# SWA's first low parts behind the first half's maxima, and four rows scaled by GpSimd at the end, in a one-core encoder step

## The chip, the cores and the metric

The kernel runs on one core of a Trainium2 chip. The metric is the device time of one execution in microseconds (us). Three runs of the kernel before took 2179.26, 2181.84 and 2182.01 us; their median is 2181.84 us. A separate execution was profiled: it took 2183.19 us, and its first and last instruction lie 2181.1 us apart. This distance is called the span, and all places in the trace are given in us from its start.

The engines are called by the profile's names: PE is TensorE (PEld its weight loads), DVE is VectorE, ACT is ScalarE, POOL is GpSimd, and SP is SyncE, which here only issues DMAs.

## The reference, cut to what matters

One step of an encoder layer for 1024 prompt tokens and 64 sample tokens (1088 in all) with 1024 features, in float32:

```
xn = rms_norm(x)
A  = retention(xn) ...                       # 4 heads, rms_norm, swish gate, w_ret_out
B  = sliding_window_attention(xn) ...        # 16 heads of 64, chunks of 64, w_swa_out
x += (sigmoid(gate_a) * A + sigmoid(gate_b) * B) @ w_mix_out
mk, mv = rms_norm(mem) @ w_mk, rms_norm(mem) @ w_mv
x += cross_attention(rms_norm(x), mk, mv)
x += (silu(h @ w_gate) * (h @ w_up)) @ w_down       # h = rms_norm(x)
y  = x * rsqrt(mean(x * x) + eps) * g_final
```

Two pieces of this matter here. In the sliding-window attention (SWA) each chunk's scores get a bias, their maximum is taken, and exp, sum and division follow. In the last line, every token's sum of squares over all 1024 features has to be there before any element of y is.

## The kernel before, in words

Features lie on the 128 partitions, as eight tiles (k = 0 to 7) of 1088 token columns. Each float32 operand of the large products is split into two fp32r parts: a high part, which is a rounded copy made by ACT, and a low part, the rest, which DVE gets by a subtraction. A product then takes three matmuls: high by high, high by low, low by high (`mm3`, lines 156 to 158; `multiply`, lines 212 to 215). The phases come one after the other: projections with retention, SWA, merging, cross-attention, and the feed-forward net, whose last part (`down`, `finish`) makes y.

The order of the instructions on each engine is fixed when the kernel is built. A scheduler places them by their place in the source; `issue_after(x)` keeps what is in its block behind the instruction x in that order, `in_order` (line 911) puts PE's work behind the last matmul, and `queued` (line 1630) does the same for DVE. An engine works off its own order strictly, and so do the DMA queues that SP, ACT and POOL issue: what stands behind a waiting instruction waits too. Tiles come from pools with a few buffers, and who takes a buffer again waits for its last reader.

**The start of SWA.** There are 17 chunks in two halves each (`swa`, `halves`). `scores` multiplies on PE (line 972), takes bias and maximum on DVE (L982, four units with an accumulator each), prepares the sinks' part on DVE (L986), and exponentiates on ACT (L988, and L990 for the sinks). Then DVE adds and inverts the denominators (L991, L992) and POOL scales (L994). `turn` transposes on PE (L949 for values, L1011 for weights), `weigh` multiplies with the values (L1035). For each half `self.marks` keeps a pair: the sinks' part on DVE and the exponential of it on ACT. The list is filled as the halves are written down, so `marks[-1]` is that of the newest half, and `marks[0]` that of the first.

Between the halves, pieces of other products fill PE. `filler` (from line 1151) gives them out: first the last head of the memory values (two token tiles, 24 matmuls each, scaled by a factor per token at line 1167, stored by POOL's DMAs at L1168 and L1169), then the product of the retention output with `w_ret_out`, for which eight gated tiles of 384 columns (`ret`) and the first weights (`wq`) need high and low parts. `first_loads` has made their high parts on ACT (L1108, L1112); `first_low` makes the ten low parts on DVE (L1120). It is called at the start of `filler`, when two halves of scores have been written down. Behind it stand the next weights (L123 on ACT and L124 on DVE), and each finished product is multiplied by its gate on DVE (L1196), which also frees its PSUM buffer, of which there are two.

**The end.** The 1088 columns form three groups: c = 0 and c = 1 with 272 columns each, and c = 2 with 544, whose sums are finished first. `finish` has 16 products left, eight for c = 0 and eight for c = 1. After each, `grow` adds it to its row of y on DVE (L1654) and ACT squares it (L1658); `gather` adds up the squares (L1663). For each group, `sums` adds over the partitions on PE with a matrix of ones (L1672), `roots` makes the factor per token (four small steps on DVE and a square root on ACT, L1757 to L1764), `spread` brings it to all partitions on PE (L1690) and ACT copies it to `rstd` (L1694). Then a row is scaled and stored in one of two ways:

- `scale`: DVE multiplies by gain and factor in one instruction (L1700), for c = 0 and most of c = 1 with the factor straight from PSUM;
- `gain` and `aside`: ACT multiplies by the gain (L1705), POOL by the factor from `rstd` (L1709).

Of group 2, rows 0 to 6 go the first way, between the products of c = 1, and row 7 the second. Of group 1, three rows go the second way. Stores are issued by SP, those of group 1 in turn by SP and ACT. Products, sums and spreads take PSUM from a pool of four bank pairs.

Of the kernel before, what the change touches and what calls it, by code (L numbers as in the profile page):

```python
# [11 lines left out]
F32 = mybir.dt.float32  # L12
F32R = mybir.dt.float32r
AF = mybir.ActivationFunctionType
ALU = mybir.AluOpType
# [4 lines left out]
P = 128  # L20
# [89 lines left out]
class Kernel:  # L110
# [616 lines left out]
    def bank(self, name):  # L727
        return self.pr.tile([P, 2, BLK], F32, tag="r", name=name)
# [386 lines left out]

    def first_low(self):

        with self.tc.issue_after(self.marks[-1][0]):
            for a, hi, lo in self.first:
                self.nc.vector.tensor_tensor(out=lo, in0=a, in1=hi.bitcast(F32), op=ALU.subtract)  # L1120

# [29 lines left out]
    def filler(self):  # L1151

        nc, tc, io = self.nc, self.tc, self.io
        if True:
            ld, rets = self.ld, self.rets
            self.first_low()
            us, h = self.first_units, H - 1
            for t in range(2):
                ps = self.dense_psum()
                for k in range(KT):  # L1160
                    x = self.ms[k][:, :, t * P:(t + 1) * P]
                    self.mm3(ps[:, :256], x[:, 0], x[:, 1], *us[k // 4][k % 4], k == 0, k == KT - 1)
                    if k == 3:
                        yield
                o = ld()[:, :256]
                with tc.high_priority():
                    self.values_out = nc.scalar.mul(o, ps[:, :256], self.mtok[:, t:t + 1]).ins
                nc.gpsimd.dma_start(self.d_mv[h, :, t, :], o)  # L1168
                nc.gpsimd.dma_start(io["o_mv"][t * P:(t + 1) * P, h * 256:(h + 1) * 256], o)  # L1169
                yield  # L1170
            self.mem.close()
            self.pw2 = self.mem.enter_context(tc.tile_pool(name="pw2", bufs=2, reuse_waits="tile", side="right"))
            with tc.issue_after(self.values_out):
                units = {0: self.first_out, 1: self.unit(io["w_ret_out"][1], KT)}
            order = [(m, c) for c in range(3) for m in range(2)] + [(m, c) for m in range(2, KT) for c in range(3)]
            halves = [range(4), range(4, KT)]
            extra = {2: (1, 0), 3: (1, 1), 5: (2, 0), 7: (2, 1)}
            step = 0
            for m, c in order:
                c0, n = CH[c]  # L1180
                if m not in units:
                    if m == 2:
                        with tc.issue_after(first[0]), tc.issue_after(first[1]):
                            units[m] = self.unit(io["w_ret_out"][m], KT)
                    else:
                        units[m] = self.unit(io["w_ret_out"][m], KT)
                u, g = units[m], ld()
                self.load(g[:, :n], self.d_gate[1][m, :, c0:c0 + n])
                for ps in self.pieces(u, rets, c0, n):
                    if step in extra:  # L1190
                        i, j = extra.pop(step)
                        self.later_operands(*CH[i], halves[j])
                    step += 1
                    if ps is None:
                        yield
                ins = nc.vector.tensor_tensor(out=g[:, :n], in0=ps, in1=g[:, :n], op=ALU.mult).ins  # L1196
                if step == 6:
                    first = self.marks[-1]
                self.store(self.d_mix[m, :, c0:c0 + n], g[:, :n])
                yield  # L1200
# [434 lines left out]
    def finish(self, y, rest):  # L1635
# [29 lines left out]
        def sums(c, *more):  # L1665
# [8 lines left out]
            r = self.np.tile([P, 5], F32, tag="rf", bufs=2, name="rs_f")[:, :len(spans)]  # L1674
            factors[c] = r, spans, ps[:, :, 0]

        def roots(c, between=None):
            r, spans, ps = factors[c]
            v = self.np.tile([P, 5], F32, tag="vf", bufs=2, name="rf_v")[:, :len(spans)]
            t = self.np.tile([P, 5], F32, tag="tf", bufs=2, name="rf_t")[:, :len(spans)]  # L1680
            self.steps(r, v, t, ps, between)
# [21 lines left out]
        def gain(c, k):  # L1703
            o = y[k][:, cols[c]]
            nc.scalar.mul(o, o, self.gains[:, 3, k:k + 1])  # L1705

        def aside(c, k, queue=nc.sync):
            o = y[k][:, cols[c]]
            nc.gpsimd.tensor_tensor(out=o, in0=o, in1=self.rstd[:, cols[c]], op=ALU.mult)  # L1709
            queue.dma_start(self.io["o_y"][k, :, cols[c]], o)  # L1710

        for j in range(2 * KT):
# [10 lines left out]
            if j == KT + 3:  # L1723
                self.in_order(lambda: sums(0))
                roots(0)
            if j == KT + 6:
                pb0 = self.in_order(lambda: spread(0, False))[:, :HC]
            if c and m < KT - 1:
                scale(2, m)
            if c and KT - 5 < m < KT - 1:  # L1730
                gain(1, rest[m][0])
            if j == 2 * KT - 2:
                gain(2, KT - 1)
                aside(2, KT - 1)
        m = rest[-1][0]
        spare = [rest[i][0] for i in range(KT - 4, KT - 1)]
        scale(0, 0, pb0)
        scale(0, 1, pb0)
        self.in_order(lambda: sums(1, squares[1, m]))
        roots(1, lambda: scale(0, 2, pb0))  # L1740
        for k in range(3, KT):
            scale(0, k, pb0)
# [91 lines left out]
```

## Time and profile before

| what | value |
| --- | --- |
| median of three runs | 2181.84 us |
| the profiled execution | 2183.19 us, span 2181.1 us |
| busy share of the span | PE 98%, DVE 71%, ACT 40%, POOL 30% |
| mean granted PE clock | 0.995 |
| bytes moved by DMA | 290.84 MB |
| first and last score matmuls of SWA | 809.3 and 970.8 us |
| PE's waits from 808 to 980 us, after the profile | 4.2 us |
| products of `finish` on PE | from 2143.8 to 2167.3 us |
| last DVE and POOL instruction ends | about 2176.9 us |

A row of the timeline gives the start, the duration, the engine, the line, the operation, the tiles written and read with their shapes, and a count where like instructions were merged. A bracket tells how long the engine had stood idle before, and what ended it. A row of the windows gives, for one stretch, the busy time of PE, PEld, DVE, ACT and POOL, the granted PE clock as a share of full speed, the busy share of the DMA engines and what they moved. Durations of one instruction include its latency, so the starts of neighbours tell the pace better.

### The profile page before, as it was taken

To read this page: it belongs to the slowest core of one execution; us is meant where nothing else is said; L and a number is where in the kernel's file an instruction comes from. 1 tells how busy PE (TensorE), PEld (TensorE's weight loads), DVE (VectorE), ACT (ScalarE), POOL (GpSimd) and SP (SyncE) were. 2 spreads that over 40 slices of the span, in tenths; PEclk is the share of its full clock that TensorE was granted. 3 is DMA by queue.
4 is the path that set the end of the run, shared out by engine and by line. 5 is a ranking of instruction groups with operands and counts; after the bars stand their busy time and mean duration, and the time that the engine had idled before them with its cause. 6 is when DMAs were issued, how large, how long until landed. Compare 5 with 4: busy or idle time off the path is not lost. (4 is left out here: it accounts for less than half of the span.)

```text
span 2181.1 us, 41848 instructions
## 1 busy us (share of the span) xinstructions
PE 2142.3 (98%) x16389; PEld 2089.0 (96%) x16389; DVE 1553.4 (71%) x2824; ACT 876.4 (40%) x1898; POOL 651.7 (30%) x498
## 2 busy tenths in 40 slices
PE   8999999999999999999999999999999999999997
PEld 8999999999999997889999999999999999999997
DVE  8996868776687658665455555768777777787688
ACT  7344424344344447553233333333322322344343
POOL 1223233342344214430000000014565555514531
PEclk9999999999999999999999999999999999999999
DMA  6434354435344467326443111422333323294433
GB/s 208 154 131 114 114 152 125 137 111 159 103 160 164 166 206 246 118 80 219 124 155 120 40 49 59 146 87 91 121 124 116 105 96 120 94 331 128 135 107 119
DMA packets 181446, 290.84 MB, mean 133 GB/s; under 512 B 40290, under 2 KB 109314, under 8 KB 181250
## 3 DMA queue, kind: packets, MB, share of 16 engines
q1 hardware_dynamic: 176130, 278.18, 40.1%
q10 hardware_dynamic: 4608, 8.36, 1.0%
q8 instruction: 129, 2.11, 0.4%
q0 software_dynamic: 512, 1.64, 0.2%
q14 instruction: 67, 0.55, 0.1%
HBM read 196.95 MB, written 91.16 MB: 132 GB/s over the span
## 5 line engine op out<-in xcount | busy, mean ns | idle before, releaser
L124 DVE TENSOR_TENSOR wq<-raw,wq 128x512 fp32r<-128x512 f32 (+1 forms) x499 | 443.9, 893 | 134.8 <-ACT wq L123 131.4
L123 ACT CAST wq<-raw 128x512 fp32r<-128x512 f32 (+1 forms) x499 | 303.1, 614 | 567.1 <-PE pq L215 223.3
L212 PE MATMUL pq<-T,wq 128*128 128x272 f32 x1832 | 492.0, 288 | 4.9 <-ACT wq L123 3.3
L213 PE MATMUL pq<-T,wq 128*128 128x272 f32 x1832 | 492.9, 289 | 0.0
L213 PE MATMUL pq<-B,wq 128*128 128x272 f32 x1592 | 428.2, 289 | 2.9 <-DVE B L124 2.6
L212 PE MATMUL pq<-B,wq 128*128 128x272 f32 x1592 | 426.6, 288 | 0.5 <-ACT B L123 0.5
L190 POOL TENSOR_TENSOR raw<-raw 128x512 f32<-128x512 f32 (+1 forms) x59 | 86.0, 1458 | 1036.5 <-DVE rs_r L301 483.0
L215 PE MATMUL pq<-T,wq 128*128 128x272 f32 x1832 | 382.8, 289 | 1.5 <-DVE wq L124 1.5
L212 PEld LDWEIGHTS pq<-T,wq 128*128 128x128 f32 x1832 | 345.0, 188 | 6.7 <-ACT wq L123 3.1
L213 PEld LDWEIGHTS pq<-T,wq 128*128 128x128 f32 x1832 | 344.9, 188 | 1.2 <-issue 1.1
L215 PE MATMUL pq<-B,wq 128*128 128x272 f32 x1592 | 332.2, 289 | 0.0
L213 PEld LDWEIGHTS pq<-B,wq 128*128 128x128 f32 x1592 | 299.5, 188 | 4.3 <-DVE B L124 4.2
L212 PEld LDWEIGHTS pq<-B,wq 128*128 128x128 f32 x1592 | 299.4, 188 | 1.4 <-ACT B L123 0.9
L215 PEld LDWEIGHTS pq<-T,wq 128*128 128x128 f32 x1832 | 290.2, 190 | 2.6 <-DVE wq L124 1.8
L215 PEld LDWEIGHTS pq<-B,wq 128*128 128x128 f32 x1592 | 252.2, 190 | 0.5 <-issue 0.4
L259 DVE TENSOR_TENSOR u<-pq,u 128x544 f32<-128x544 f32 x177 | 127.2, 719 | 95.5 <-PE pq L215 95.4
L193 POOL TENSOR_TENSOR raw<-raw 128x512 f32<-128x512 f32 (+1 forms) x59 | 80.8, 1370 | 91.4 <-DVE wq L124 81.5
L598 DVE TENSOR_TENSOR stage<-pq,u 128x544 f32<-128x544 f32 x112 | 80.3, 717 | 36.9 <-PE pq L215 32.4
L191 POOL TENSOR_TENSOR raw<-raw 128x512 f32<-128x512 f32 (+1 forms) x59 | 88.8, 1505 | 3.6
L196 POOL TENSOR_TENSOR raw<-raw 128x512 f32<-128x512 f32 (+1 forms) x59 | 84.0, 1423 | 4.4
L1483 POOL TENSOR_TENSOR stage<-stage,rstd_f 128x544 f32<-128x544 f32 x40 | 63.9, 1607 | 39.1 <-ACT stage L1482 39.1
L156 PE MATMUL pd<-xc,wq 128*128 128x256 f32 (+1 forms) x256 | 74.5, 291 | 0.0
(383 smaller groups left out, 4548.4 us busy)
## 6 DMA issues: line engine op xcount, KB each, us to landing
hl<-d_op SPq DMA_DIRECT2D x85, 272.0 KB, 5.3
d_qkv<-stage SPq DMA_DIRECT2D x44, 272.0 KB, 2.7
d_op<-stage SPq DMA_DIRECT2D x44, 272.0 KB, 2.1
d_op<-ht SPq DMA_DIRECT2D x44, 272.0 KB, 3.3
raw<-w_gate SPq DMA_DIRECT2D x22, 512.0 KB, 3.6
raw<-w_up SPq DMA_DIRECT2D x22, 512.0 KB, 4.0
raw<-w_down SPq DMA_DIRECT2D x16, 512.0 KB, 4.8
d_gate<-stage ACTq DMA_DIRECT2D x28, 272.0 KB, 3.0
```

The source lines that it names most:

```text
L123: self.last_cast = self.nc.scalar.copy(hi, src).ins
L124: return self.nc.vector.tensor_tensor(out=lo, in0=src, in1=hi.bitcast(F32), op=ALU.subtract).ins
L156: mm(ps, wh, xh, start=start, stop=False)
L190: tt(out=a11, in0=a11, in1=a21, op=sub)
L191: tt(out=a21, in0=a21, in1=a22, op=add)
L193: tt(out=a11, in0=a22, in1=a11, op=sub)
L196: tt(out=a12, in0=a12, in1=a11, op=sub)
L212: mm(ps[:, c, :HC], w[:, 0, ks], x[:, 0, cs], start=start, stop=False)
L213: mm(ps[:, c, :HC], w[:, 0, ks], x[:, 1, cs], start=False, stop=False)
L215: self.last_mm = mm(ps[:, c, :HC], w[:, 1, ks], x[:, 0, c * HC:(c + 1) * HC], start=False, stop=stop).ins
L259: add = lambda out, a, b: nc.vector.tensor_tensor(out=out, in0=a, in1=b, op=ALU.add)
L598: nc.vector.tensor_tensor(out=o, in0=ps, in1=sb, op=ALU.add)
```

## The change

Three things are changed.

1. `first_low` comes behind the first half's mark instead of the newest one, and the memory values of the last head are scaled by DVE instead of ACT.
2. Of group 2, rows 0 to 3 are scaled by DVE as before. Rows 4 to 7 get their gain on ACT, and POOL scales all four of them, behind a copy of one column that reads `rstd` after the last gather of group 1. Their stores go to SP's queue, among those of group 0.
3. Three matmuls of the matrix of ones by itself stand between the last product and the sums of group 1, and five between these sums and the spread, all into a PSUM tile of their own.

```diff
     def first_low(self):
-        with self.tc.issue_after(self.marks[-1][0]):
+        with self.tc.issue_after(self.marks[0][0]):
             for a, hi, lo in self.first:
...
                 with tc.high_priority():
-                    self.values_out = nc.scalar.mul(o, ps[:, :256], self.mtok[:, t:t + 1]).ins
+                    self.values_out = nc.vector.tensor_scalar(o, ps[:, :256], self.mtok[:, t:t + 1], None, ALU.mult).ins
...
+        def warm(ps, count):
+            for i in range(count):
+                self.last_mm = nc.tensor.matmul(ps[:, :P], self.ones, self.ones, start=True, stop=True).ins
...
             if j == KT + 6:
+                spin = bank()
                 pb0 = self.in_order(lambda: spread(0, False))[:, :HC]
-            if c and m < KT - 1:
+            if c and m < KT - 4:
                 scale(2, m)
             if c and KT - 5 < m < KT - 1:
                 gain(1, rest[m][0])
-            if j == 2 * KT - 2:
-                gain(2, KT - 1)
-                aside(2, KT - 1)
+            if c and 2 <= m < KT - 2:
+                gain(2, m + 2)
         m = rest[-1][0]
         spare = [rest[i][0] for i in range(KT - 4, KT - 1)]
+        flag = self.np.tile([P, 1], F32, tag="flag", bufs=1, name="flag")
+        behind = nc.gpsimd.tensor_copy(flag, self.rstd[:, cols[1]][:, :1]).ins
+        with self.tc.issue_after(behind):
+            for k in range(KT - 4, KT):
+                aside(2, k)
         scale(0, 0, pb0)
         scale(0, 1, pb0)
+        self.in_order(lambda: warm(spin, 3))
         self.in_order(lambda: sums(1, squares[1, m]))
+        self.in_order(lambda: warm(spin, 5))
         roots(1, lambda: scale(0, 2, pb0))
```

## The prediction, made before the changed kernel was run

> **What bounds the kernel now.** First the page: how full is each engine?
>
> ```profile
> span 2181.1 us, 41848 instructions
> PE 2142.3 (98%) x16389; PEld 2089.0 (96%) x16389; DVE 1553.4 (71%) x2824; ACT 876.4 (40%) x1898; POOL 651.7 (30%) x498
> ```
>
> TensorE (PE) works 98% of the span, so time is won only where it waits or runs slowly, and behind its last matmul. In the order of instructions that the two kernels are built with, they differ at two places only: the start of SWA and the last 50 us. I read the timeline there, engine by engine. At SWA, DVE first, then PE:
>
> ```profile
> 817.92 0.16 DVE L991 TENSOR_TENSOR den<-den,es 128x4 f32<-128x4 f32 x1 [6.79 <-ACT es L990]
> 819.49 0.68 DVE L1120 TENSOR_TENSOR wq<-raw,wq 128x512 fp32r<-128x512 f32 x1
> 820.09 1.95 DVE L1120 TENSOR_TENSOR ret<-swin,ret 128x384 fp32r<-128x384 f32 x4
> 822.57 1.95 DVE L1120 TENSOR_TENSOR ret<-swin,ret 128x384 fp32r<-128x384 f32 x4
> 824.73 1.70 DVE L124 TENSOR_TENSOR wq<-raw,wq 128x512 fp32r<-128x512 f32 x2
> 826.34 0.55 DVE L1196 TENSOR_TENSOR swin<-pd,swin 128x384 f32<-128x384 f32 x1
> ```
>
> ```profile
> 820.27 0.44 PE L156 MATMUL pd<-ret,wq 128*128 128x384 f32 x1
> 825.28 0.71 PE L972 MATMUL pss<-swin,swin 64*128 64x128 f32 x8
> 827.03 0.41 PE L156 MATMUL pd<-ret,wq 128*128 128x384 f32 x1 [0.35 <-DVE swin L1196]
> 835.11 0.33 PE L157 MATMUL pd<-ret,wq 128*128 128x384 f32 x1
> 836.85 0.34 PE L158 MATMUL pd<-ret,wq 128*128 128x384 f32 x1
> 838.59 0.92 PE L972 MATMUL pss<-swin,swin 64*128 64x192 f32 x8 [1.40 <-DVE nm L982]
> ```
>
> A bracket holds the idle time ahead of an instruction and what ended it. DVE stands idle for 6.79 us, then works off ten low parts (L1120) from 819.49 to 824.5, and only then turns to what PE needs. PE pays twice: its 24 matmuls from 820.27 keep step with DVE, and at 827.03 it waits for L1196.
>
> The end, in the order PE, DVE, POOL:
>
> ```profile
> 2167.05 0.29 PE L158 MATMUL pq<-T,wb 128*128 128x272 f32 x1
> 2169.74 0.38 PE L1672 MATMUL pq<-ones,rstd 128*128 128x2 f32 x2 [2.40 <-DVE rstd L1663]
> 2172.58 1.65 PE L1690 MATMUL pq<-ident,rs_f 128*128 128x128 f32 x6 [1.33 <-DVE rs_f L1764]
> ```
>
> ```profile
> 2165.42 0.78 DVE L1700 SCALAR_TENSOR_TENSOR y<-y,gains,rstd 128x544 f32<-128x544 f32 x1
> 2168.91 0.43 DVE L1654 TENSOR_TENSOR y<-pq,y 128x272 f32<-128x272 f32 x1
> 2172.44 2.12 DVE L1700 SCALAR_TENSOR_TENSOR y<-y,gains,pq 128x272 f32<-128x272 f32 x5
> ```
>
> ```profile
> 2157.49 1.37 POOL L1709 TENSOR_TENSOR y<-y,rstd 128x544 f32<-128x544 f32 x1 [22.88 <-ACT rstd L1694]
> 2174.73 2.19 POOL L1709 TENSOR_TENSOR y<-y,rstd 128x272 f32<-128x272 f32 x3 [15.86 <-ACT rstd L1694]
> ```
>
> PE is through at 2167.34. The sums wait until 2169.74 for DVE, which has three rows of 544 columns in its queue, the first at 2165.42, ahead of the last grow (L1654) at 2168.91. The windows show the DMA engines (last three columns: granted PE clock, DMA share, GB/s):
>
> ```profile
> 2172.60:2174.30 1.70, 1.63 (x6) 1.33 (x6) 1.70 (x5) 0.04 (x1) 0.00 (x0) 0.50 0.52 166
> 2177.00:2177.50 0.50, 0.00 (x0) 0.00 (x0) 0.00 (x0) 0.00 (x0) 0.00 (x0) 0.50 1.04 359
> 2179.00:2179.50 0.50, 0.00 (x0) 0.00 (x0) 0.00 (x0) 0.00 (x0) 0.00 (x0) 0.50 0.78 272
> ```
>
> After the last arithmetic (2176.9) the DMA engines are full, at 359 GB/s, until about 2179.4. The end is thus already a matter of bytes.
>
> **The change part by part.** *SWA.* The ten low parts now follow the first half's maxima, that is, 811.1. They need ACT's high parts, of which the weights' two come late, and the order of the built kernel puts two new things around them: DVE takes over the two scalings L1167, and on ACT two casts (L123) move ahead of the second half's exponentials.
>
> ```profile
> 811.58 0.60 ACT L1112 CAST wq<-raw 128x512 fp32r<-128x512 f32 x1
> 813.89 0.60 ACT L1112 CAST wq<-raw 128x512 fp32r<-128x512 f32 x1
> 819.67 0.19 ACT L990 ACTIVATE es<-es 128x4 f32<-128x4 f32 x1
> 820.44 0.47 ACT L1167 ACTIVATE swin<-pd,mtok 128x256 f32<-128x256 f32 x1 [0.22 <-PE pd L158]
> 820.81 1.14 ACT L123 CAST wq<-raw 128x512 fp32r<-128x512 f32 x2
> 818.71 0.28 PE L158 MATMUL pd<-wq,ms 128*128 128x256 f32 x1
> 829.93 0.63 PE L1011 MATMUL pp<-ident,t 128*64 128x128 f32 x4
> ```
>
> The ten take 824.5 - 819.49 = 5.0 us. The first cast that they need ends at 812.2, the second, for the sixth of them, at 814.5, so they run from 812.2 to about 817.2, inside the idle time that lasts until 817.92. Nothing of DVE moves back. Then PE's 24 matmuls run at their own pace: (836.85 - 835.11) / 10 = 0.174 us each, 24 x 0.174 = 4.2, with the change of stage 4.35 instead of 825.28 - 820.27 = 5.01: **-0.66**. DVE's L1196 follows PE at once, about 824.6 instead of 826.34, and the next half's maxima begin 1.5 us earlier; so the wait of 0.35 at 827.03 goes, and with it the slower first matmul behind a wait (0.41 against 0.33) and the time in which the array fills again, 0.2 together as an estimate: **-0.55**.
> What is late next? L1167 on DVE is not shown in the trace: ACT's 0.47 bounds it above and DVE's 0.16 for four columns (817.92) below; I take 0.4, near the other 256-wide one. Its second copy waits for PE until 820.4 as ACT's does now, and ahead of L1196 lie only the two L124 (1.7 or less) and the small divisions: DVE is free by 822.8, 1.8 us before 824.6. On ACT the second cast waits for the matmul at 818.71 (its weight buffer), so the two end near 819.6, and the exponentials, whose last step is at 819.67 now, end near 821.3. PE transposes that half at 829.93: over 7 us of room after POOL's scaling. POOL issues two of its value stores ahead of scaling the first half, which PE wants only some 5 us later. SP's ten loads queued behind these buffers start some 7 us earlier; they hide as before.
> The wait of 1.40 us at 838.59 stays: DVE and ACT work there in a chain that starts from PE's own scores, so all of it shifts together. SWA: **-1.2 us**, with 0 and -1.9 as ends (nothing; half of the 1.40 gone as well).
>
> *The end.* Three 544-wide rows leave DVE. The last grow then follows PE, at 2167.40 instead of 2168.91: **-1.5** for the sums and what hangs on them. ACT gets three more gains of the kind at 2148.13:
>
> ```profile
> 2148.13 0.75 ACT L1705 ACTIVATE y<-y,gains 128x544 f32<-128x544 f32 x1
> 2138.54 0.66 ACT L1576 ACTIVATE sq<-y 128x544 f32<-128x544 f32 x1 [2.15 <-DVE y L1565]
> 2165.39 0.83 PE L1690 MATMUL pq<-ident,rs_f 128*128 128x128 f32 x6
> 2158.89 0.34 SPq L1710 DMA_DIRECT2D o_y<-y  x1
> 2159.50:2160.00 0.50, 0.50 (x6) 0.50 (x6) 0.50 (x2) 0.00 (x0) 0.00 (x0) 1.00 0.54 213
> ```
>
> They go into gaps like the 2.15 us ahead of 2138.54 and cost nothing; 0.75 each if one held up a cast that PE waits for.
> The ones matmuls: two passes of 0.138 (0.83 / 6) each, so three are done by 2168.2, before the sums start at 2168.23, and five last 1.4 us behind the sums' 1.5, to 2171.15, where DVE's four small steps end too (2171.0). They cost about 0.1. Their tile takes one of four PSUM pairs, so PE's last product gets the pair of the product two before; DVE frees it with the grow that takes the place of the row at 2165.42 and ends at 2165.85, while PE comes to it some 0.58 behind the spread's start at 2165.39: no wait, or 0.1. The clock was 0.50 in the spread of 1.65 us and full in the like one of 0.83; it should stay full, -0.8. But DVE has five 272-wide rows (2.12) between its last small step and the spread rows, until 2173.0, and the spread is there at 2172.4: the 0.8 is hidden. Its last row moves with that by 1.5 us.
> POOL now starts behind the last gather (2168.2) with a one-column copy, bounded by 0 and 0.3, and four rows of 1.37: it comes free at 2173.8, and its three short rows (2.19) end at 2176.0 instead of 2176.9. So by engines alone the end would move by **-0.9**.
> Now the bytes. Row stores for 4 x 272 KB, which went out between 2159 and 2170, become ready at 2169.7, 2171.1, 2172.5 and 2173.8. SP issues in order, so the 136 KB rows queue behind them. From 2169.7 on there remain 4 x 272 + 6 x 136 + 8 x 136 = 2992 KB = 3.06 MB, at 0.36 MB/us 8.5 us. Bytes flow 0.8 us after an issue (2158.89 to 2159.7, as a share of 0.54 in half a microsecond says), so from 2170.5 to 2179.0, with some 0.3 of holes at the first rows to 2179.3: as good as the 2179.4 now. The end gains **-0.1**, bounded by -0.9 (engines alone) and +0.5 (POOL's flag and rows at their longest).
>
> Sum: -1.2 - 0.1 = -1.3. The profiled execution took 2183.19 us around its span of 2181.1 and becomes 2181.9; it lies 1.35 above the median of 2181.84, which becomes **2180.5**.
>
> **The rivals.** *The bytes don't bind*: POOL's last row sets the end, -1.2 - 0.9 = -2.1, 2179.7.
>
> ```profile
> 2169.70:2174.00 4.30, 2.92 (x18) 2.77 (x18) 3.42 (x12) 0.30 (x2) 0.00 (x0) 0.84 0.51 176
> ```
>
> For it: the DMA engines had half of this stretch free, 4.3 x (360 - 176) = 0.8 MB of room. Against: the four rows are 1.1 MB.
> *SWA gives nothing*: the two waits are made good at 838.59, where PE would stand longer: -0.1, 2181.7. For it: DVE's backlog is what ended that wait. Against: the backlog itself starts earlier.
> *The wait at 838.59 goes as well*, because all that DVE had put off is done by then: -1.2 - 1.4 - 0.9 = -3.5, 2178.3; with the scatter of a median of three runs (2179.26 to 2182.01) half of this is beyond 0.2%.
> *Slower, the clock*: ACT's casts ahead of the exponentials wait for PE. If the half isn't normalised when PE wants to transpose it (829.93), PE stands there.
>
> ```profile
> 810.99 1.12 PE L972 MATMUL pss<-swin,swin 64*128 64x64 f32 x8 [1.01 <-DVE nm L982]
> 810.50:817.30 6.80, 6.31 (x32) 6.20 (x33) 0.60 (x7) 6.75 (x17) 1.62 (x3) 0.51 0.64 224
> ```
>
> Around the short wait at 810.99 the clock fell to half for these 6.8 us. A wait of 1.5 us with 6.8 us at half clock behind it costs 1.5 + 3.4 = 4.9: with nothing won elsewhere, 2186.7. It decides from the point at which the exponentials slip by more than 7 us; the count above says under 2. The Trainium skill (TensorE: Matmul & The Clock Gate, What's actually happening) says the gate closes after an idle window of about 3.4 us; by that rule alone this rival could not be, and the warm-up matmuls at the end would guard against nothing. The trace speaks against it: half clock after waits of 1.01 and of 2.40 and 1.33 us.
> *POOL's four rows drag* beside DVE: at 2 us each they end at 2176.4, its last rows at 2178.6, the stores at 2180.5: +1.1 there, 2181.7 in all. In the row at 2174.73 the short rows took 0.73 beside DVE's. The Trainium skill (GPSIMD Engine Reference, Key points) has the two engines collide only where DVE reads two SBUF inputs or runs in a two-port mode; DVE's rows there read the factor from PSUM, and the trace agrees: 0.73 is what 1.37 gives for half the columns.
>
> **How the numbers follow.** Forecast 0.50; bytes don't bind 0.14; SWA gives nothing 0.12; that wait goes 0.14; clock 0.05; POOL drags 0.05. A difference of 0.2% (4.4 us) is about what a measurement of this kernel tells from none. Faster by more: half of the fourth, 0.07. Slower by more: the clock, 0.05. Within: 0.88. Range for 8 in 10: from 2178.0 (just under the fourth) to 2183.0 (nothing at SWA, +0.5 at the end, one gain in a cast's way); it leaves out the clock and the far half of the fourth.
>
> **What would show it.** L1120 between 811 and 818 and no DVE idle of 6.79; the matmuls from 820.27 to the scores in 4.4; no wait at L1196; 1.40 still at 838.59's place. At the end: last grow 0.1 behind PE, clock 1.00 in the spread, spread 0.83, POOL without a gap, DMA share near 1 from 2171 on and an end within 0.5 us of now. The forecast is wrong if PE waits anew at the transposes, if the wait at 838.59 changes by more than 0.5, or if the DMA share has holes after 2172.

## The result, and the profile after

The changed kernel takes 2190.55 us, the median of five runs (2188.15 to 2192.36), against 2181.64 us for the kernel before (2179.26 to 2182.01). The ratio is 1.0041, with a 95% interval of 1.0030 to 1.0052: 8.9 us slower, where 2180.5 us (2178.0 to 2183.0) was forecast. The head of the page after:

```profile
span 2188.5 us, 41882 instructions
PE 2152.1 (98%) x16405; PEld 2099.1 (96%) x16405; DVE 1547.0 (71%) x2823; ACT 877.9 (40%) x1899; POOL 654.7 (30%) x502
```

PE is busy 9.8 us longer with 16 passes more, the eight ones matmuls, which at 0.138 us are 2.2 us. The granted clock is the same (0.996 against 0.995). So PE does part of the rest of its work at a lower pace. To find where, take the same matmul in both traces, counted from the first: its start after less its start before, in us.

| matmul at (before) | 118 | 400 | 626 | 798 | 829 | 1026 | 1200 | 1494 | 1800 | 2144 | end of span |
| --- | --- | --- | --- | --- | --- | --- | --- | --- | --- | --- | --- |
| later by | -3.2 | -1.5 | 0.0 | 1.9 | -0.7 | -1.6 | -1.3 | 0.0 | 2.8 | 5.1 | 7.5 |

The 3.2 us at 118 are no gain of the edits: between 75 and 100 us the clock was 0.95 before and 1.00 after, and one wait for DVE (at L487, for L478) took 2.0 us before and 0.2 after. At SWA (798 to 829) the changed kernel gains 2.6 us, half of it ahead of the edited place (from 810 to 814 the clock was 0.58 before and 1.00 after), and at the end it loses. But the largest piece is lost where nothing was edited: 3.2 us from 118 to 626, 1.9 us from 626 to 798, and 5.1 us from 1494 to 2144. In the last of these it is lost evenly, 0.44 or 0.45 us in each 50 us, but for two stretches in which the kernel before lost some 0.4 us itself. In all three most matmuls have 272 columns.

The windows of before, then of after, show the feed-forward net's first 400 us (PE's busy time and its matmuls, clock, DMA share, GB/s):

```profile
1500.00:1900.00 400.00, 400.00 (x3217) 1.00 0.34 113
```

```profile
1500.00:1900.00 400.00, 400.00 (x3189) 1.00 0.35 113
```

PE stands nowhere in either, the clock is full, the DMA engines carry the same, and yet 28 matmuls fewer fit in: 125.4 instead of 124.3 ns each. The starts of single matmuls show a fixed rhythm, as a product's matmuls come in sixes (L212, L213, L212, L213, L215, L215). Over some 530 sixes from 1500 to 1900 us, before takes 746 or 747 ns for each, after 753 or 754 (means 746.7 and 753.3). A wait for another engine would hardly keep such a rhythm. 10272 matmuls have this width and these lines (the page's groups of L212, L213 and L215), so the 1.1 ns are worth up to 11 us; the three stretches lose 10.2.

What differs between the kernels for these matmuls is not their order, which is the same, but their operands' places. The new tile `flag` stands in the pool `norm`, which lies in SBUF (the memory of 128 partitions that the engines compute from) ahead of the weights' pool. It takes 32 bytes per partition, and all that is allocated behind it on the left side, the split weights `wq` among it, lies 32 bytes higher. The rings with the moving operands are allocated from the right side and stay.

SWA in the profile after, first DVE, then PE:

```profile
812.93 0.16 DVE L986 TENSOR_TENSOR es<-sinks,nm 128x4 f32<-128x4 f32 x1
813.02 0.69 DVE L1120 TENSOR_TENSOR wq<-raw,wq 128x512 fp32r<-128x512 f32 x1
816.10 1.95 DVE L1120 TENSOR_TENSOR ret<-swin,ret 128x384 fp32r<-128x384 f32 x4
817.98 0.15 DVE L991 TENSOR_TENSOR den<-den,es 128x4 f32<-128x4 f32 x1
825.26 0.56 DVE L1196 TENSOR_TENSOR swin<-pd,swin 128x384 f32<-128x384 f32 x1 [2.20 <-PE pd L158]
```

```profile
820.89 0.34 PE L156 MATMUL pd<-ret,wq 128*128 128x384 f32 x1
825.16 0.72 PE L972 MATMUL pss<-swin,swin 64*128 64x128 f32 x8
837.91 0.92 PE L972 MATMUL pss<-swin,swin 64*128 64x192 f32 x8 [1.38 <-DVE nm L982]
```

The ten low parts stand right behind the first maxima and are done by 817.98. The 24 matmuls take 4.27 us, L1196 now waits for PE and nothing waits for L1196, and the wait of 1.40 has stayed at 1.38. From 820.89 to 837.91 are 17.02 us, where before took 838.59 - 820.27 = 18.32.

The end, in the order PE, DVE, POOL:

```profile
2172.19 0.29 PE L158 MATMUL pq<-T,wb 128*128 128x272 f32 x1
2173.36 0.38 PE L1672 MATMUL pq<-ones,rstd 128*128 128x2 f32 x2 [0.21 <-DVE rstd L1663]
2178.79 1.10 PE L1694 MATMUL pq<-ident,rs_f 128*128 128x128 f32 x6 [2.71 <-DVE rs_f L1775]
```

```profile
2172.52 0.44 DVE L1654 TENSOR_TENSOR y<-pq,y 128x272 f32<-128x272 f32 x1 [0.54 <-PE pq L158]
2175.38 0.17 DVE L1772 RECIPROCAL rs_f<-rs_f 128x3 f32<-128x3 f32 x1
2175.58 0.58 DVE L1773 TENSOR_TENSOR rf_t<-rs_f 128x3 f32<-128x3 f32 x1
2176.19 1.25 DVE L1774 SCALAR_TENSOR_TENSOR rf_t<-rf_t,rf_v 128x3 f32<-128x3 f32 x1
2177.48 1.25 DVE L1775 SCALAR_TENSOR_TENSOR rs_f<-rf_t,rs_f 128x3 f32<-128x3 f32 x1
```

```profile
2173.50 5.21 POOL L1713 TENSOR_TENSOR y<-y,rstd 128x544 f32<-128x544 f32 x4
```

The sums come early, as forecast: 2173.36 is 1.17 us behind the last product, where before needed 2169.74 - 2167.05 = 2.69. Then three steps of three columns each, which took 0.16 us, last 0.58, 1.25 and 1.25 beside POOL's rows, and PE waits 2.71 us for them. Each of the three ends within 0.02 us of one of POOL's rows (at 2176.14, 2177.43 and 2178.72 in the trace). The windows show the DMA engines full from 2177.0 on and again behind the spread, with a hole between (a share of 0.25 from 2178.5 to 2179.5, and of 0.44 in the microsecond after):

```profile
2177.00:2178.50 1.50, 0.00 (x0) 0.00 (x0) 1.47 (x2) 0.00 (x0) 1.50 (x2) 1.00 1.02 372
2181.50:2185.50 4.00, 0.00 (x0) 0.00 (x0) 1.31 (x4) 0.00 (x0) 1.13 (x2) 0.50 1.01 348
```

Ahead of 2177.0 there is another hole, though three stores have been issued by then. SP's rows, the hole, and, from the list of the DMA queues between 2174.40 and 2176.10, the one that the profile calls "instruction" (packets, MB, share of 16 engines):

```profile
2173.74 0.33 SPq L1705 DMA_DIRECT2D o_y<-rstd_f  x1
2174.17 0.38 SPq L1705 DMA_DIRECT2D o_y<-y  x1
2174.87 1.50 SPq L1714 DMA_DIRECT2D o_y<-y  x1
```

```profile
2175.50:2176.80 1.30, 0.58 (x6) 0.39 (x4) 1.23 (x3) 0.00 (x0) 1.30 (x2) 1.00 0.07 18
q8 instruction: 1, 0.02, 5.5%
```

The three stores land 3.5 us after their issue. In the kernel before, the stores of the same first two rows landed after 1.8. One packet of 16 KB on the instruction queue keeps one of the 16 DMA engines busy from 2174.50 to 2176.01 (5.5% of 16 times 1.70 us are 1.5 us). Until 2176.8 the share is then 0.07, about one engine of 16. The third issue takes 1.50 us, where most take 0.33 to 0.41.

The span ends 16.36 us behind the start of the last product's last matmul, where before took 14.02. Below, the end is always counted from there.

### The profile page after: what moved, and what is told of

Read it like the earlier page. It is cut to its first block, busy times and chain, and to the rows that moved or that the text cites. A ratio compares the mean times of both kernels' runs of the same rounds, so it can differ in the third digit from the quotient of the medians.

```text
span 2188.5 us, 41882 instructions
## 1 busy us (share of the span) xinstructions
PE 2152.1 (98%) x16405; PEld 2099.1 (96%) x16405; DVE 1547.0 (71%) x2823; ACT 877.9 (40%) x1899; POOL 654.7 (30%) x502
## 4 chain that ended last, share of the span: by engine, by line
PE 83%; DVE 9%; DMA 4%; ACT 2%; issue 1%; POOL 1%; SPq 0%; DVEq 0%; POOLq 0%; ACTq 0%
PE pq L213 16%; PE pq L212 16%; PE pq L215 16%; PE pd L156 8%; PE pd L158 8%; PE pd L157 8%; DVE wq L124 2%; PE pss L972 1%; PE pout L1035 1%; DMA raw<-w_k 1%; PE pp L1011 1%; DVE stage L630 0%; DVE stage L598 0%; DVE u L259 0%; DMA raw<-w_sq 0%
## 5 line engine op out<-in xcount | busy, mean ns | idle before, releaser
L212 PE MATMUL pq<-T,wq 128*128 128x272 f32 x1832 | 496.1, 289 | 4.8 <-ACT wq L123 3.0
L213 PE MATMUL pq<-T,wq 128*128 128x272 f32 x1832 | 498.5, 289 | 0.0
L213 PE MATMUL pq<-B,wq 128*128 128x272 f32 x1592 | 432.0, 289 | 2.7 <-DVE B L124 2.6
L212 PE MATMUL pq<-B,wq 128*128 128x272 f32 x1592 | 429.3, 288 | 0.4 <-ACT B L123 0.4
L215 PE MATMUL pq<-T,wq 128*128 128x272 f32 x1832 | 379.5, 287 | 1.3 <-DVE wq L124 1.3
L212 PEld LDWEIGHTS pq<-T,wq 128*128 128x128 f32 x1832 | 344.8, 188 | 6.8 <-ACT wq L123 3.2
L213 PEld LDWEIGHTS pq<-T,wq 128*128 128x128 f32 x1832 | 347.3, 190 | 1.2 <-issue 1.1
L215 PE MATMUL pq<-B,wq 128*128 128x272 f32 x1592 | 328.5, 287 | 0.0
L213 PEld LDWEIGHTS pq<-B,wq 128*128 128x128 f32 x1592 | 301.1, 189 | 3.7 <-DVE B L124 3.6
L212 PEld LDWEIGHTS pq<-B,wq 128*128 128x128 f32 x1592 | 298.6, 188 | 1.3 <-ACT B L123 0.8
L215 PEld LDWEIGHTS pq<-T,wq 128*128 128x128 f32 x1832 | 289.9, 188 | 2.5 <-DVE wq L124 1.6
L215 PEld LDWEIGHTS pq<-B,wq 128*128 128x128 f32 x1592 | 251.2, 187 | 0.5 <-issue 0.4
```

Of the source, the lines that this page charges most:

```text
L212: mm(ps[:, c, :HC], w[:, 0, ks], x[:, 0, cs], start=start, stop=False)
L213: mm(ps[:, c, :HC], w[:, 0, ks], x[:, 1, cs], start=False, stop=False)
L215: self.last_mm = mm(ps[:, c, :HC], w[:, 1, ks], x[:, 0, c * HC:(c + 1) * HC], start=False, stop=stop).ins
```

## The experiments

Each run's time stands beside runs of the kernel before on the same chip. "Six" is the mean time of six matmuls from 1500 to 1900 us, worked out from the starts as above.

### Is it the place?

e1, the kernel before with a tile that nothing uses:

```diff
-            self.sinks = cp.tile([P, NPAIR], F32, name="sinks")
+            self.sinks = cp.tile([P, NPAIR], F32, name="sinks"); pad = cp.tile([P, 8], F32, name="pad")
```

> The kernel before, with one unused tile of 32 bytes per partition ahead of the weights' pool: no instruction is added or moved, but every tile that is allocated on the left side of SBUF, the split weights (wq) among them, lies 32 bytes higher, as it does in the changed kernel (wq from 16320 to 16352, that is from a multiple of 64 to 32 beyond one). Theory (the address costs the changed kernel its time, since the new one-column tile flag shifts these tiles): 2190.5 us (2188 to 2193), and six matmuls of 272 columns in the feed-forward net take 753 ns instead of 746. Rival (the edits themselves cost it: the ones matmuls, POOL's rows, DVE's scaling, the order on ACT): 2181.6 us as before, 746 ns.

2192.62 us against 2181.80, ratio 1.0049 (1.0031 to 1.0067), six in 753.3 ns. Its window:

```profile
1500.00:1900.00 400.00, 400.00 (x3188) 1.00 0.35 115
```

e2, the changed kernel with its flag elsewhere:

```diff
-            self.rtok = cp.tile([P, 9], F32, name="rtok")
+            rtok = cp.tile([P, 10], F32, name="rtok"); self.rtok, self.flag = rtok[:, :9], rtok[:, 9:]
...
-        flag = self.np.tile([P, 1], F32, tag="flag", bufs=1, name="flag")
+        flag = self.flag
```

> The changed kernel with its one-column copy written into a free tenth column of rtok, which has room in its 64 bytes: the same instructions in the same order, but all tiles lie where they lay before. Theory (address): 2180.5 us (2178.5 to 2182), the forecast of the prediction, 746 ns for six matmuls. Rival (the edits themselves): 2190.5 us, 753 ns.

2180.70 us against 2181.80, ratio 0.9995 (0.9983 to 1.0007).

```profile
1500.00:1900.00 400.00, 400.00 (x3217) 1.00 0.34 112
```

A tile that no instruction touches costs as much as the whole change, and the change without the new place costs nothing that can be measured. The edits themselves are ruled out as the cause.

### Which places?

e3 moves the rings instead, e4 both sides:

```diff
-                self.rings = [Ring(...
+                rpad = sctx.enter_context(tc.tile_pool(name="rpad", bufs=1, reuse_waits="tile", side="right")).tile([P, 8], F32, name="rpad"); self.rings = [Ring(...
```

```diff
-            self.rtok = cp.tile([P, 9], F32, name="rtok")
+            rtok = cp.tile([P, 11], F32, name="rtok"); self.rtok = rtok[:, :9]
...
-            self.mtok = cp.tile([P, 2], F32, name="mtok")
+            self.mtok = rtok[:, 9:]
```

e4 has both diffs.

> The kernel before, with an unused tile of 32 bytes ahead of the rings on the right side: the moving operands of the matmuls in the rings lie 32 bytes lower, on multiples of 64 (B11 from 159712 to 159680); the weights stay on multiples of 64. No instruction is added or moved. If only the weights' own address counts: 2181.6 us, 746 ns. If the address of each operand counts by itself: faster, about 2173 us, 739 ns. If it is the relation of the two (slow when both lie the same way modulo 64): 2190 us, 753 ns.

> As the run before this one, and mtok placed in two free columns of rtok, so that the left side lies 32 bytes lower: weights 32 beyond a multiple of 64 (wq at 16288), moving operands in the rings on multiples of 64. If only the weights' own address counts: 2190 us, 753 ns. If each operand counts by itself: 2181.6 us, 746 ns. If it is the relation of the two: 2181.6 us, 746 ns.

e3: 2191.11 us against 2181.80, ratio 1.0039 (1.0026 to 1.0053), six in 753.3. e4: 2181.76, ratio 1.0000 (0.9988 to 1.0012), six in 746.7. Weights on a multiple of 64 are slow in e3 and fast before; so it is no operand's own alignment, but how the two lie to each other. To see whether alike or apart modulo 64 is the rule, e9 and e11 move the left side by 64, e11 with e3's diff as well:

```diff
-        r = self.np.tile([P, 4], F32, tag="r", bufs=2, name="rs_r")[:, :len(spans)]
+        r = self.np.tile([P, 4], F32, tag="rr", bufs=2, name="rs_r")[:, :len(spans)]
```

> The kernel before, with two small tiles that are never alive together (rs_r and rr) put in the same buffers, so that the left side lies 64 bytes lower: the weights stay on a multiple of 64 but lie 0 instead of 64 beyond a multiple of 128; the rings stay. No instruction is added or moved. If alike or apart modulo 64 decides (the four full kernels): 2181.8 us, 746 ns for six matmuls. If finer bits decide as well (the groups of the run with pairs alone gave 746.7 for the weights shifted by 64 and 760 for 128, where 753.3 stood without shift): another of the values 750, 753 or 760, which is 2187, 2191 or 2200 us (9.4 us were 7 ns).

> The left side 64 bytes lower as in the run two before, and the rings 32 lower: weights and moving operands both on multiples of 64, but the weights 0 and the first half of a moving operand 64 beyond a multiple of 128. If alike or apart modulo 64 decides: 2191 us, 753 ns. If finer bits decide: another of 746, 750 or 760.

e9: 2192.77 us against 2181.25, ratio 1.0057 (1.0039 to 1.0075), six in 753.3. e11: 2175.88, ratio 0.9976 (0.9965 to 0.9987), six in 743.3. Both go against the rule modulo 64: it falls. What fits all runs is the distance from weights to rings. Two more runs test that: e15 makes e11's distance at other addresses (e4's second diff alone), e14 adds 128 to the distance of the changed kernel (e4's second diff and e9's).

> The kernel before with mtok in free columns of rtok: the left side 32 bytes lower (wq at 16288), the rings at their old places: the same distance as in e11 at addresses that are both 32 higher. No instruction is added or moved. If the distance alone decides: 743.5 ns and 2176 us as there. If absolute addresses count: another pace.

> The kernel before with mtok in free columns of rtok and rs_r in rr's buffers: the left side 96 bytes lower (wq at 16224), the rings at their old places, so that the weights lie 128 bytes further from them than in the changed kernel. If the pace repeats every 128 bytes of distance: 753.4 ns and about 2191 us, as with no distance. If it repeats at 256 or not at all: another of 743.5 to 760 ns (2176 to 2200 us).

e15: 2175.79 us against 2180.68, ratio 0.9980 (0.9971 to 0.9989). e14: 2192.84, ratio 1.0051 (1.0038 to 1.0064). e15's window:

```profile
1500.00:1900.00 400.00, 400.00 (x3231) 1.00 0.35 114
```

| run | `wq` | ring (`B11`) | ring less `wq`, modulo 128 | matmuls in 1500 to 1900 | six, ns | us |
| --- | --- | --- | --- | --- | --- | --- |
| before | 16320 | 159712 | 32 | 3217 | 746.7 | 2181.64 |
| e4 | 16288 | 159680 | 32 | 3216 | 746.7 | 2181.76 |
| after | 16352 | 159712 | 0 | 3189 | 753.3 | 2190.55 |
| e1 | 16352 | 159712 | 0 | 3188 | 753.3 | 2192.62 |
| e3 | 16320 | 159680 | 0 | 3188 | 753.3 | 2191.11 |
| e14 | 16224 | 159712 | 0 | 3188 | 753.3 | 2192.84 |
| e9 | 16256 | 159712 | 96 | 3188 | 753.3 | 2192.77 |
| e11 | 16256 | 159680 | 64 | 3231 | 743.3 | 2175.88 |
| e15 | 16288 | 159712 | 64 | 3231 | 743.3 | 2175.79 |

(All buffers of `wq` and all slots of the rings lie multiples of 128 apart, so one number stands for all. The second group of 272 columns begins 1088 bytes behind the first, which is 64 more modulo 128, so every six has matmuls at two distances; the table gives that of the first.) Equal distance gave equal pace each time, to 0.1 ns.

e10 asks whether the weights are what counts, or something else on the left side:

```diff
-                self.wp = self.left.enter_context(tc.tile_pool(name="weights", bufs=2, reuse_waits="tile"))
+                self.wp = self.left.enter_context(tc.tile_pool(name="weights", bufs=2, reuse_waits="tile")); lpad = self.left.enter_context(tc.tile_pool(name="lpad", bufs=1, reuse_waits="tile")).tile([P, 8], F32, name="lpad")
```

> The kernel before, with an unused tile of 32 bytes behind the weights' pool: everything else on the left side lies 32 bytes higher, as in the changed kernel, but raw and the five buffers wq lie where they lay before (the sixth one, which takes 64 of 533 weights, lies 32 higher). Theory (the weights that PE loads are what counts): 2182 to 2183 us, 746 ns but where the sixth buffer is in use. Rival (operands of DVE, ACT or the DMAs in the other pools): 2191 us.

2184.88 us against 2181.25, ratio 1.0016 (1.0006 to 1.0025), six in 749.1 on average: 379 of 533 sixes take 746 or 747, the others 749 to 761. This is between the two expectations, 2 us above the theory's. Most sixes keep the old rhythm although everything else on the left side but `raw` and the five buffers moved. The disturbed ones, 154, come in 22 runs of seven, which take about 749, 760, 756, 753, 757, 761 and 751 ns. In the order of the built kernel, the second to fifth of each run multiply with weights of the sixth buffer, and no other six of this window does. So it is the weights, six by six. The displaced buffer also upsets the six before it and the two behind. One run of seven takes 60 ns more than seven undisturbed sixes, where four sixes at the slow pace would take 27 more. With 48 of its 64 weights in products of 272 columns that is 2.9 us, against the 3.6 measured.

e5 leaves the computation out and takes PE alone:

```diff
+            def group(name, w, x, n, count=16):
+                ps = pp.tile([P, 2, 512], F32, tag="q", name=name)
+                for r in range(count):
+                    k, first, last = r % 4, r == 0, r == count - 1
+                    at = w + k * P
...
+            for name, w, x, n in [("w_zero_x_zero", 0, 0, 272), ("w_four_x_zero", 1, 0, 272), ...]:
+                group(name, w, x, n)
```

> A kernel that leaves the whole computation out: 60 warming matmuls, then groups of 96 matmuls of one weights' tile and one moving tile in the order of the feed-forward net (six per 128 features), where only the place of the weights or of the moving operand in its tile is shifted by some bytes, and then the width. Both tiles begin 32 beyond a multiple of 64, so that a group without shift has both alike modulo 64. By the table of the four runs before: alike (no shift, 64, 128, both shifted by the same) 753 ns for six matmuls of 272 columns, apart by 32 or 96 bytes 746 ns, whichever of the two is shifted. Open, and what the run is for: shifts of 4, 8, 16 and 48 bytes. If the half of a 64-byte line counts (one bit of the address): 753 at 4 to 16, 746 at 48. If the distance counts by degrees: 753 falling towards 746 between 0 and 32. 384 and 512 columns: no difference, since there the columns and not the loads of the weights set the pace; 256 and below: a difference as large or larger.

The timeline of e5, first matmul of some groups (names are cut from the left; "two" is a shift of 32, "ero" none, the words at the end are the columns):

```profile
88.99 0.29 PE L380 MATMUL w_sixtyfour_x_zero<-xt,wt 128*128 128x272 f32 x1
100.94 0.29 PE L380 MATMUL w_ninetysix_x_zero<-xt,wt 128*128 128x272 f32 x1
112.94 0.29 PE L380 MATMUL w_onetwentyeight_x_zero<-xt,wt 128*128 128x272 f32 x1
...
276.14 0.30 PE L380 MATMUL ero_x_zero_n_twofiftysix<-xt,wt 128*128 128x256 f32 x1
287.67 0.28 PE L380 MATMUL two_x_zero_n_twofiftysix<-xt,wt 128*128 128x256 f32 x1
299.02 0.31 PE L380 MATMUL ero_x_zero_n_threetwenty<-xt,wt 128*128 128x320 f32 x1
```

A group is 16 sixes: shifted by 64 they take 11.95 / 16 = 0.747 us, by 96 0.750. Without a group's first six, which varies, the mean was 753.3 ns without shift and 759.8 at 128. With 256 columns 11.53 / 16 = 0.721 stands against 0.709 us. So PE alone, with no other engine at work but for a copy and a store behind each group, shows the effect. But its rule is not the table's: no shift and 128 differ here, and one distance gave different paces at different places (both operands at one place: 753.3, 753.0 and 750.0 ns; the moving one 32 further: 750.0, 753.3 and 746.6). At 128, 192 (670 ns both), 320 (880 both) and 384 columns (1040 both) the place made no difference, at 512 the shifted group was the slower one (1400 against 1360). The expectation was right that PE's own two operands suffice, and wrong on the values and on 512 columns.

### What are the edits worth?

e6 has the first two hunks of the change alone, e7 the rest with e2's flag.

> The kernel before with the two edits at SWA alone (first low parts behind the first half's mark, memory values scaled by DVE), all tiles at their old places. The forecast's step: 1.2 us less between PE's matmuls of 815 us and those of 829 us, no wait at L1196, nothing given back by 840 us; 2180.5 us in all. From the runs before (e2 and the changed kernel gained 2.14 and 1.79 there against the kernel before, three kernels without the edit 0.71, 0.20 and 0.66) rather 1.6. Rival (SWA gives nothing): no difference from the kernels without the edit by 840 us.

> The kernel before with the edits at the end alone (four rows for POOL, its flag in a free column of rtok, the ones matmuls), all tiles at their old places. The forecast's step: the end 0.1 us earlier after PE's last product. Theory from the trace of e2: DVE's last three small steps between the sums and the spread read two operands from SBUF, and each stands until POOL has finished one of its rows (0.57, 1.25 and 1.25 us instead of 0.16), so that the spread starts some 6.5 us after PE's last product instead of 4 and the last store lands 14.5 us after it instead of 12.3 to 13.4: 1 to 2 us more than the kernel before, about 2183. Rival (the new rows' bytes alone set the end): the same lateness without the long small steps.

e6: 2180.80 us against 2182.04, ratio 0.9994 (0.9984 to 1.0004). e7: 2183.39, ratio 1.0011 (1.0001 to 1.0020). The medians hardly tell these apart, the traces do. From the first of the 24 matmuls to the scores behind the wait of 1.40, the six profiled kernels with SWA's edit took 16.98 to 17.09 us; the ten without it 17.12 to 18.37, mean 18.0, with before's 18.32 near the upper end. So the edit gains 1.0 us on average and 1.3 against the profiled run of before. From the start of the last product's last matmul to the end of the span, after, e2, e7 and e13 took 16.32 to 16.36 us, the kernels with the old end mostly 13.99 to 14.90 (e14: 15.46): the edits at the end lose about 2. By the traces about 1 us is lost, not 1.3 won. e2's median, 1.1 below the kernel before, does not show this loss, but its interval allows it.

e8 takes POOL's hold off DVE's steps:

```diff
-        q(lambda: nc.vector.reciprocal(out, out))
-        q(lambda: nc.vector.tensor_tensor(out=t, in0=out, in1=out, op=ALU.mult))
-        q(lambda: stt(t, t, -0.5, v, ALU.mult, ALU.mult))
-        q(lambda: stt(out, t, 1.5, out, ALU.add, ALU.mult))
+        r, w = (out, out) if room is None else (room[:, :v.shape[1]], v); q(lambda: nc.vector.reciprocal(r, out))
+        q(lambda: nc.vector.tensor_tensor(out=t, in0=w, in1=r, op=ALU.mult))
+        q(lambda: stt(t, t, -0.5, v if room is None else r, ALU.mult, ALU.mult))
+        q(lambda: stt(out, t, 1.5, r, ALU.add, ALU.mult))
```

Here `room` is the free half of the PSUM pair into which the ones matmuls write.

> The changed kernel with all tiles at their old places (as e2), and group 1's last three small steps rewritten so that each reads one operand from PSUM and one from SBUF (v times r, times r, plus 1.5 times r, with r the reciprocal in a free bank): the same count of instructions. Theory (a DVE instruction with two operands in SBUF waits for POOL's row, one with an operand in PSUM does not): the four steps take 0.16 to 0.2 us each, beside POOL's rows at 1.3 us each as before; the spread starts 2 us earlier, its clock stays at full speed (0.83 instead of 1.65 us), and the last store lands 1.0 us earlier than in e2 (0.5 to 1.5; the bytes bind behind that): about 2179.7. Rival (the steps are slow for another reason, such as POOL's rows as such or PE's ones matmuls in the same PSUM tile): still 0.57, 1.25 and 1.25 us, and 2180.7.

2181.00 us against 2182.04, ratio 0.9992 (0.9982 to 1.0001), so the forecast of 1.0 us less than e2 does not show in the medians. In its trace, DVE and POOL:

```profile
2167.11 0.18 DVE L1772 RECIPROCAL pq<-rs_f 128x3 f32<-128x3 f32 x1 [0.73 <-PE pq L1679]
2167.33 0.16 DVE L1773 TENSOR_TENSOR rf_t<-rf_v,pq 128x3 f32<-128x3 f32 x1
2167.52 0.16 DVE L1774 SCALAR_TENSOR_TENSOR rf_t<-rf_t,pq 128x3 f32<-128x3 f32 x1
2167.71 0.16 DVE L1775 SCALAR_TENSOR_TENSOR rs_f<-rf_t,pq 128x3 f32<-128x3 f32 x1
```

```profile
2164.43 7.38 POOL L1713 TENSOR_TENSOR y<-y,rstd 128x544 f32<-128x544 f32 x7
```

Beside the same rows of POOL the steps take 0.16 us each. The end comes 14.86 us after the last product's last matmul instead of 16.32: 1.46 less. So reading two operands from SBUF beside POOL was what held them. The Trainium skill (SBUF — State Buffer, SBUF: two separate sides) states it: a DVE instruction with two SBUF inputs and a GpSimd instruction that reads SBUF exclude each other for a whole instruction, and the loser is blocked. The trace agrees: 1.25 us for each of two steps is about one of POOL's rows, 5.21 / 4 = 1.30.

e12 also takes away the 0.73 us wait in e8's first row, by giving the steps the second half of the sums' own PSUM pair (against e8):

```diff
...
-            ps = bank()[:, :2 * len(spans)].rearrange("p (t two) -> p t two", two=2)
+            pair = self.bank_pair(); rooms[c] = pair[:, 1, :]; ps = pair[:, 0, :2 * len(spans)].rearrange("p (t two) -> p t two", two=2)
...
-        roots(1, lambda: scale(0, 2, pb0), room)
+        roots(1, lambda: scale(0, 2, pb0), rooms[1])
```

> As the run with the steps in PSUM, but their PSUM tile is the second half of the sums' own pair, where that run had them in the tile of the ones matmuls and DVE's first step waited 0.73 us for the last of these. The steps then begin 0.7 us earlier, the spread starts 4.8 us after the start of PE's last product instead of 5.5 (7.8 in the changed kernel with the old places, 6.8 in the kernel before), at full clock. If the engines set the end, the last store lands 0.7 us earlier, 13.1 us after that product instead of 13.8; if the bytes do, as the forecast had it, 13.8 stays.

2181.98 us against 2181.25, ratio 1.0004 (0.9992 to 1.0017). The spread's last matmul starts 4.66 us after that of the last product (e8: 5.47), but the span ends at 14.65 instead of 14.86: of 0.81 us that the engines won, 0.21 are left. From there on the bytes bind, as e8's windows already show for the 8.5 us up to its last bytes:

```profile
2167.50:2176.00 8.50, 0.93 (x6) 0.74 (x6) 4.40 (x12) 0.39 (x1) 4.30 (x5) 0.79 1.01 356
```

e13 puts the whole change at the best distance, with `flag` and `mtok` both in `rtok`:

```diff
-            self.rtok = cp.tile([P, 9], F32, name="rtok")
+            rtok = cp.tile([P, 12], F32, name="rtok"); self.rtok, self.flag = rtok[:, :9], rtok[:, 11:]
...
-            self.mtok = cp.tile([P, 2], F32, name="mtok")
+            self.mtok = rtok[:, 9:11]
```

> The changed kernel with flag and mtok in free columns of rtok, so that the left side lies 32 bytes lower than in the kernel before, and the weights (wq at 16288) 64 modulo 128 below the rings (159712): the distance of the fastest run so far, e11. If the distance alone decides, and the edits are worth what they were at the old places (1.1 us, from 2181.8 to 2180.7): 2174.8 us, 743.5 ns for six matmuls. If the absolute addresses count too: another pace.

2176.81 us against 2180.68, ratio 0.9981 (0.9971 to 0.9990), six in 743.3. It beats both kernels, and is no better than the kernel before at the same distance (e15, 2175.79). The expected 1.1 us from the edits did not appear; the two medians differ by 1 us the other way, within their scatter.

## Why the prediction was wrong, point by point

**The step that failed** is the first one: "In the order of instructions that the two kernels are built with, they differ at two places only". That is true, and nothing follows from it for the other 2100 us. The prediction took the same order of instructions for the same time, and priced the flag as an instruction ("a one-column copy, bounded by 0 and 0.3") but not as a tile. Its 32 bytes change how the weights lie to the moving operands, which costs 9.3 to 10.8 us alone (e3, e1). No rival, no row and no bound of the range had room for this, so the forecast missed the sign as well.

**SWA was right**, in mechanism and nearly in size: -1.2 against -1.3 in the profiled pair (its two terms -0.66 and -0.55 against -0.74 and -0.56) and -1.0 as a mean. All four marks came: low parts from 813, 24 matmuls in 4.27 us (4.4), no wait at L1196, 1.38 left. What the prediction could not see from one trace is that the stretch varies by itself, by up to 1.25 us without any edit.

**The end was wrong in two terms.** The last grow follows PE at once, as forecast (0.33 us from the start of the last product's last matmul), and POOL runs without a gap. But "DVE's four small steps end too (2171.0)" failed: they end 6.5 us after the last product's last matmul instead of 4, since three of them read two operands from SBUF beside POOL's new rows. The prediction had weighed this collision, in the rival "POOL's four rows drag", and had looked only at the rows, which read PSUM; it never asked it of the four steps. So POOL did not drag, DVE did. With the spread late, the ones matmuls guard nothing: in after the spread took 1.10 us with the clock falling, in e2, e7 and e13 1.65, in e8 0.93. The upper bound of +0.5 was passed (some +2, of which 1.46 are these steps).

The other term is "Bytes flow 0.8 us after an issue". The first of POOL's rows was issued at 2174.87, and its bytes came at 2176.8. So the marks named for the DMA engines did not come: a share near 1 from 2171 on and no holes after 2172 (here 5.1 us later). In all six kernels with the new end the 16 KB packet on the instruction queue falls 2.1 to 2.4 us behind the start of the last product's last matmul, and the first two or three stores land 3.1 to 3.5 us after their issue. In eight of the ten kernels with the old end no such packet falls in the 14.8 us behind that matmul, and no store issued in the first 8 of them took over 3. In the two others, e1 and e14, it falls at 4.6 and 8.6, two stores took 3.4 to 3.8 each, and e14 has the latest end of the ten. e8 and e12 have the packet as well, so it fits the 0.8 us by which e8 still ends later than before (14.86 against 14.02). No run moved the packet: that it costs these 0.8 is argued, not shown, and why it comes early with the new end is open.

**That the bytes bind** was right once they flow: e12 shows it. Hence the end cannot win much by faster engines, and the rival "the bytes don't bind" would have failed even without the steps. "SWA gives nothing" and "that wait goes too" fell with the trace; the slower clock at SWA did not come (1.00 from 820 on).

What stays open is the law behind the pace. In the fifteen kernels of this shape whose weights all lie at one distance, this distance modulo 128 told it exactly; in PE alone, with shorter runs and other tiles, it did not. Why 64 is best is not shown.

## What to carry to other kernels

Before costing a change, compare the addresses of the two built kernels as well as their order: a new tile of a few bytes ahead of a matmul's operands can outweigh the whole edit, and moving a pool by 32 bytes, with an unused tile or by joining two small ones, is a cheap probe for both a loss and a gain. When the loss is spread evenly over stretches that were not edited, count instructions in a long window without waits instead of looking at the edited place. And where GpSimd gets work, look through everything that VectorE does meanwhile for instructions with two SBUF operands, the smallest ones too.

## What the runs showed of the hardware

- The time of a 272-column fp32r matmul with its own weights depends on where weights and moving operand lie: 743.3, 746.7 or 753.3 ns for six, in a rhythm that holds for hundreds of microseconds. In this kernel that is 2175.8 to 2192.8 us (e15, e14) with the same instructions.
- In PE alone, matmuls of 128 and 192 columns take the same 111.7 ns (670 / 6), 320 columns 146.7 and 384 columns 173.3, at both places tried; the place counts at 256 and 272, and again at 512 (e5).
- A VectorE instruction on three columns can take 1.25 us: about as long as the GpSimd row beside it, 1.30 (after).
- Stores of 136 KB landed 1.8 us after their issue in the kernel before. Where a 16 KB packet of the queue called "instruction" fell in between, the first two behind the last product took 3.1 to 3.5 us (after, e2, e7, e8, e12, e13), and two took 3.4 to 3.8 in e1 and e14.
